# Hybrid trunk on one core: input quarters ahead of weight splits, and part of GpSimd's sine chain ahead of the first norm's factors

## The chip, the cores and the metric

The kernel runs on one core of a Trainium2 chip. The metric is the device time of one execution in microseconds; before the change it was 993.73 (median of three runs, 992.82 to 994.16). All times below are microseconds unless marked ns. TensorE is PE, VectorE is DVE, ScalarE is ACT, GpSimd is POOL, SyncE is SP, which issues most of the DMAs.

## The reference, cut to what matters

A decoder trunk of two layers over 256 tokens of width 1024, batch 1. Each layer is half a gated feed-forward block, a token mixer, and another half block:

```
for layer in range(2):
    h = h + 0.5 * swiglu(rms_norm(h, ffn_norm[layer, 0]), w_gate, w_up, w_down)
    h = h + mixer(rms_norm(h, mix_norm[layer]))        # layer 0: S5 state space, layer 1: block attention
    h = h + 0.5 * swiglu(rms_norm(h, ffn_norm[layer, 1]), w_gate, w_up, w_down)

rms_norm(x, g) = x * rsqrt(mean(x * x) + 1e-6) * g
swiglu(h)      = (silu(h @ w_gate) * (h @ w_up)) @ w_down          # inner width 2816
```

The S5 mixer needs tables that depend on its parameters alone. Two of their steps matter here:

```
dt  = exp(log_dt)
lam = exp(a_re * dt) * (cos(a_im * dt) + i * sin(a_im * dt))
```

and powers of lam after that.

## The kernel before

**Arithmetic.** All matrix products are float32 in three passes: a weight is split into a rounded part `whi` (ScalarE, line 84) and a rest `wlo` (VectorE, line 85), activations are split the same way into `xa` high and low halves, and TensorE adds high x high, low x high and high x low. Weights stream through three raw buffers of 1 MB (`Stream`, `RAW = 3`). A *unit* is 1 MB; it is split in two halves, numbered in order of use (split 0, 1, 2, ...). Only when both halves of a unit are split is its buffer free, and then SP issues the load of the unit three further on. `st.pump()` issues the next split if its data was asked for long enough ago.

**Order.** There is no scheduler: instructions go to each engine in the order in which the program text emits them, and each engine works through its queue in that order. Work for other engines is placed between the matmuls by lists of functions ("hooks") that run when the emission reaches a place.

**The front.** The first feed-forward half is `f00`. Its input x comes in four column *quarters* of 256. `quarter(q)` (line 1322) transposes a quarter on TensorE (line 1331, four transposes into PSUM tiles pA1 and pA3, one buffer each), scales and rounds it on ScalarE (line 1338, two instructions) and forms the rest on VectorE (line 1339, two instructions). The next quarter's transposes write the same two PSUM tiles, so they wait until VectorE has read the last ones. `gu0` (line 457) multiplies the quarters with the first gate and up weights: eight groups of six matmuls (line 471), for quarter q and token half t in the order (0,0), (0,1), (1,0), ..., (3,1). Ahead of each group it runs the hooks of `first` (line 1384), and then `fill(1.4)`, which moves a clock of slots and, from slot 9 on (that is from group (3,0)), advances the table generator `tab`.

**The norm.** The norm's factor is applied late. `square(t, n)` (line 1351) sums squares of half rows on ScalarE; after the fourth, `factors` (line 1355) makes the mean and x^-0.5 with one refinement step on GpSimd: seven instructions, lines 1356, 1357 and 304 to 308, result `rn`. In the product after gu0 (`gu(1, 0)`), `to_rows` (line 1361, ahead of its second group) transposes `rn` on TensorE, VectorE copies it, and `to_columns` (line 1368) transposes it back. Only then do `gated(0, 0)` and `gated(0, 1)` make the first activations (`sg` on ScalarE, line 478; `act` on VectorE, line 482), and `tr` transposes each (line 495) and splits it (`ah` line 497, `al` line 498).

**The tables.** `tables` (line 618) is a generator; each `next(tab)` emits its text to the next `yield`. Advance 1 is the exponent of dt on ScalarE (`dtb`, line 659). Advance 2 has three small transposes on TensorE (lines 662 to 664) and on VectorE the copy to `prm`, two reductions and `are` (lines 666 to 674). Advance 3 has `mag` and `rho` on ScalarE (lines 676, 677). Advance 4 has a transpose and copy for `dT` (lines 681, 682) and, on GpSimd through the helpers `pt` (line 685) and `pts` (lines 689, 691), the *sine chain*: fourteen instructions that reduce the angle and square it (lines 722 to 735: e0, e1, den, aim, q, y, y2), then the two polynomials `sc` (lines 736 to 743), then doublings (line 747) up to `s4`, `c4`. Later `e_init` (line 696) copies `c4` and `s4` on VectorE (lines 700, 701) into the power table `E`, and its steps (line 703, through line 626) follow, with splits between them. `pre` is eight loads of S5 parameters (`bn`, line 647), issued on SP at group (1,1).

Of the kernel before, what the change touches and what calls it, by code (L numbers as in the profile page):

```python
# [13 lines left out]
OP = mybir.AluOpType  # L14
# [11 lines left out]
TWO_PI = 2.0 * math.pi  # L26
MAGIC = 12582912.0
# [91 lines left out]
def trunk_kernel(ctx: ExitStack, tc, x, ffn_norm, ffn_w_gate, ffn_w_up, ffn_w_down, mix_norm,  # L119
# [3 lines left out]
    nc = tc.nc  # L123
# [13 lines left out]
    def psR():  # L137
        return pp.tile([128, 512], F32, name="pR", tag="R", bufs=2)

    def psA(i):  # L140
        return pp.tile([128, 512], F32, name=f"pA{i}", tag=f"A{i}", bufs=1)
# [93 lines left out]
    ident = cst[:, 0:128]  # L235
# [30 lines left out]
    if "s5" in phases:  # L266
# [5 lines left out]
        dnat = tabp.tile([8, 128], F32, name="dnat")  # L272
# [4 lines left out]
    st = Stream(nc, units, rp, hp)  # L277
# [37 lines left out]
    def home(pool, ph):  # L315

        xa = pool.tile([128, 4224], F32R, name="xa")
        v = xa[:, XO[ph]:XO[ph] + 4096].rearrange("p (i k c) -> p i k c", i=2, c=256)
        return v[:, 0], v[:, 1]
# [298 lines left out]
    def tables(tp):  # L618

        V, P = nc.vector, nc.gpsimd  # L620

        def T(name, *shape):
            return tp.tile([128] + list(shape), F32, name=name)
# [37 lines left out]
        ps = psR()  # L661
# [9 lines left out]
        dT = T("dT", 8)  # L671
        ar, ai, dt = prm[:, 0, :], prm[:, 1, :], prm[:, 2, :]
        are, aim, mag = T("are", 32), T("aim", 32), T("mag", 32)
# [1 line left out]
        yield  # L675
        nc.scalar.activation(mag, are, AF.Exp)
        nc.scalar.activation(rho, are, AF.Exp, scale=4.0)
        yield

        ps = psR()  # L680
        nc.tensor.transpose(ps[:, 0:8], dnat, ident[0:8, 0:8])
        V.tensor_copy(dT, ps[:, 0:8])

        def pt(o, a, b, op):
            P.tensor_tensor(o, a, b, op=op)  # L685

        def pts(o, a, s1, op0, s2=None, op1=None):
            if op1 is None:
                P.tensor_scalar(o, a, s1, None, op0=op0)
            else:  # L690
                P.tensor_scalar(o, a, s1, s2, op0=op0, op1=op1)

        z0, z1 = T("z0", 1024), T("z1", 1024)
        E = T("e", 2, 16, 65)
# [21 lines left out]
        def e_store(hf):  # L716
            nc.gpsimd.dma_start(dE[hf], E.rearrange("p i q c -> p (i q c)"))

        q, y, y2, e0, e1, den = (T(n, 32) for n in ("q", "y", "y2", "e0", "e1", "den"))
        sc = T("sc", 2, 32)  # L720
        sn, cs = sc[:, 0], sc[:, 1]
        pt(e0, ar, ar, OP.mult)
        pt(e1, ai, ai, OP.mult)
        pt(den, e0, e1, OP.add)
        pt(aim, ai, dt, OP.mult)
        pts(q, aim, 1.0 / TWO_PI, OP.mult, MAGIC, OP.add)
        pts(q, q, MAGIC, OP.subtract)
        c1 = 6.28125
        c2 = float(np.floor((TWO_PI - c1) * 2 ** 20) / 2 ** 20)
        c3 = TWO_PI - c1 - c2  # L730
        for k, c in enumerate((c1, c2, c3)):
            pts(e0, q, c, OP.mult)
            pt(y, y if k else aim, e0, OP.subtract)
        pts(y, y, 0.5, OP.mult)
        pt(y2, y, y, OP.mult)
        for k, n in enumerate(range(15, 1, -2)):
            if k:
                pt(sc, sc, cf7[:, k, :, None].to_broadcast([128, 2, 32]), OP.add)
# [562 lines left out]

    pre = []
    tab = tables(tabp) if "s5" in phases else iter(())
    next(tab, None)
    slot = [0]
# [16 lines left out]
    def quarter(q, mid=lambda: None):  # L1322

        if not X:
            X[phases[0], "x"] = True
            X["h"], X["l"] = home(XP[0], phases[0])
        pv = [psA(1 + 2 * k)[:, 0:256] for k in range(2)]
        for k in range(2):
            for t in range(2):
                c = (2 * q + k) * 128  # L1330
                nc.tensor.transpose(pv[k][:, t * 128:(t + 1) * 128].rearrange("p (s i) -> p i s", s=4),
                                    xn[t][:, c:c + 128], ident)
            if k == 0:
                mid()
        for k in range(2):
            g = gT[:, 2 * q + k:2 * q + k + 1]
            xh, xl = (X[p][:, 2 * q + k, :] for p in "hl")
            nc.scalar.activation(xh, pv[k], AF.Identity, scale=g)
            nc.vector.scalar_tensor_tensor(xl, pv[k], g, xh.bitcast(F32), op0=OP.mult, op1=OP.subtract)
# [11 lines left out]
    def square(t, n):  # L1351
        sq = sp.tile([128, 512], mybir.dt.bfloat16, name="sq", tag="sq", bufs=1)
        nc.scalar.activation(sq, xn[t][:, n * 512:(n + 1) * 512], AF.Square, accum_out=ss4[:, t, n:n + 1])
# [24 lines left out]
    ps = psR()  # L1378
    for a in ("h",) * 4 + ("l",) * 7:
# [1 line left out]
    st.pump()  # L1381
    next(tab, None)
    square(0, 0)
    first = {(0, 1): [st.pump, lambda: next(tab, None), lambda: quarter(1), lambda: square(1, 0)],
             (1, 0): [lambda: next(tab, None), lambda: quarter(2), st.pump, lambda: square(0, 1)],
             (1, 1): pre,
             (2, 0): [lambda: quarter(3), st.pump, lambda: square(1, 1), factors],
             (3, 0): [st.pump], (3, 1): [st.pump, lambda: warm(AF.Silu)]}
# [63 lines left out]
```

## Time and profile before

| | us |
|---|---|
| median of three runs | 993.73 (992.82 to 994.16) |
| the profiled execution | 993.93 |
| its span | 991.9 |
| TensorE busy | 973.8 (98%) |
| VectorE busy | 703.3 (71%) |
| ScalarE busy | 559.2 (56%) |
| GpSimd busy | 192.1 (19%) |

How to read the rows that follow. A timeline row has start, duration, engine, line of the kernel, operation, what it writes and reads, its shape and a count of merged instructions; in brackets stands the engine's idle time before it and what ended it. A waits row has the engine that waited and what for, then the sum, the number and the longest of these waits. A windows row has a stretch, its length, then busy time and instructions of PE, PE's weight loads, DVE, ACT and POOL, and then the granted TensorE clock, the share of the DMA engines and GB/s. The chain of work that ended last shows by which engines the span is bound:

```profile
PE 84%; DVE 7%; POOL 3%; issue 2%; ACT 2%; DMA 1%; SPq 0%; ACTq 0%; DVEq 0%; POOLq 0%
```

### The profile page before, as it was taken

The numbers are of one execution on the slowest core, as the hardware profiler recorded it, in microseconds if no ns is written. First come the engines' busy times: TensorE is split into PE (matmuls) and PEld (weight loads), VectorE is DVE, ScalarE is ACT, GpSimd is POOL, SyncE is SP. The second block draws the span as 40 slices with busy tenths as digits, with TensorE's granted clock in tenths as the row PEclk, the third lists the DMA queues.
The fourth block names the chain that finished last, engine by engine and source line by source line (L and its number), as shares of the span: only waits on it lengthen the run. The fifth ranks groups of instructions, "written<-read, shape, count | busy, mean of one in ns | idle before, by whom it ended". The sixth has DMA issues, their size and how long they took to land.

```text
span 991.9 us, 17175 instructions
## 1 busy us (share of the span) xinstructions
PE 973.8 (98%) x6695; PEld 866.0 (87%) x6695; DVE 703.3 (71%) x1148; ACT 559.2 (56%) x997; POOL 192.1 (19%) x361
## 2 busy tenths in 40 slices
PE   9999999999799999999999999999999999999998
PEld 7778888888687999999999999998888899999997
DVE  5799777768978776666667766665689667766662
ACT  6646666553255665555545555554898655655540
POOL 4882554414730100000010000000441010000000
PEclk9999999999999999999999999999999999999999
DMA  8978877886656565656536655554445446756531
GB/s 235 277 261 250 293 264 237 301 332 216 236 171 190 193 212 172 211 170 213 170 120 220 216 202 181 194 182 137 131 167 170 157 143 218 248 170 213 170 128 42
DMA packets 140000, 198.71 MB, mean 200 GB/s; under 512 B 18232, under 2 KB 111504, under 8 KB 139664
## 3 DMA queue, kind: packets, MB, share of 16 engines
q1 hardware_dynamic: 133808, 184.32, 56.2%
q0 software_dynamic: 5536, 12.71, 3.6%
q8 instruction: 52, 0.85, 0.4%
q10 hardware_dynamic: 576, 0.61, 0.3%
q14 instruction: 28, 0.23, 0.1%
HBM read 183.89 MB, written 13.66 MB: 199 GB/s over the span
## 4 chain that ended last, share of the span: by engine, by line
PE 84%; DVE 7%; POOL 3%; issue 2%; ACT 2%; DMA 1%; SPq 0%; ACTq 0%; DVEq 0%; POOLq 0%
PE pM L551 12%; PE pM L552 12%; PE pM L553 12%; PE pA L397 9%; PE pA L399 9%; PE pA L398 9%; PE pM L397 5%; PE pM L398 5%; PE pM L399 5%; DVE wlo L85 2%; DVE zo L1010 1%; POOL sc L685 1%; PE pR L331 1%; ACT whi L84 1%; PE pR L861 1%
## 5 line engine op out<-in xcount | busy, mean ns | idle before, releaser
L551 PE MATMUL pM<-xa,whi 128*128 128x256 f32 x1056 | 295.7, 280 | 0.0
L552 PE MATMUL pM<-xa,whi 128*128 128x256 f32 x1056 | 294.9, 279 | 0.0
L553 PE MATMUL pM<-xa,wlo 128*128 128x256 f32 x1056 | 294.7, 279 | 0.0
L91 DVE SCALAR_TENSOR_TENSOR wlo<-raw,gT,whi 128x512 fp32r<-128x512 f32 x328 | 228.2, 748 | 70.5 <-ACT whi L90 70.3
L85 DVE TENSOR_TENSOR wlo<-raw,whi 128x1024 fp32r<-128x1024 f32 (+1 forms) x157 | 191.4, 1234 | 55.6 <-ACT whi L84 54.7
L90 ACT ACTIVATE whi<-raw,gT 128x512 fp32r<-128x512 f32 x328 | 213.7, 711 | 19.6 <-PE pA L399 14.6
L552 PEld LDWEIGHTS pM<-xa,whi 128*128 128x128 f32 x1056 | 198.5, 188 | 2.6
L551 PEld LDWEIGHTS pM<-xa,whi 128*128 128x128 f32 x1056 | 198.5, 188 | 2.3
L553 PEld LDWEIGHTS pM<-xa,wlo 128*128 128x128 f32 x1056 | 198.5, 188 | 0.0
L84 ACT ACTIVATE whi<-raw 128x1024 fp32r<-128x1024 f32 (+1 forms) x157 | 161.1, 1049 | 29.1 <-PE pA L399 8.0
L397 PE MATMUL pA<-whi,ah 128*128 128x512 f32 x352 | 138.8, 394 | 0.0
L398 PE MATMUL pA<-wlo,ah 128*128 128x512 f32 x352 | 137.6, 391 | 0.0
L399 PE MATMUL pA<-whi,al 128*128 128x512 f32 x352 | 137.6, 391 | 0.0
L566 ACT ACTIVATE sg<-gr 128x256 f32<-128x256 f32 x66 | 27.6, 418 | 165.8 <-DVE gr L563 165.8
L397 PE MATMUL pM<-whi,xa 128*128 128x512 f32 x288 | 119.5, 415 | 0.0
L398 PE MATMUL pM<-wlo,xa 128*128 128x512 f32 x288 | 113.1, 393 | 0.1
L399 PE MATMUL pM<-whi,xa 128*128 128x512 f32 x288 | 112.7, 391 | 0.0
L346 POOL TENSOR_TENSOR ms<-ss 128x1 f32<-128x1 f32 x10 | 1.9, 193 | 472.1 <-ACT sq L343 472.1
L399 PEld LDWEIGHTS pA<-whi,al 128*128 128x128 f32 x352 | 66.1, 188 | 14.3
L397 PEld LDWEIGHTS pA<-whi,ah 128*128 128x128 f32 x352 | 66.1, 188 | 11.6
L398 PEld LDWEIGHTS pA<-wlo,ah 128*128 128x128 f32 x352 | 66.2, 188 | 11.3
L563 DVE TENSOR_TENSOR gr<-pM,rrow 128x512 f32<-128x512 f32 x66 | 45.5, 689 | 40.9 <-PE pM L553 40.8
(263 smaller groups left out, 1232.5 us busy)
## 6 DMA issues: line engine op xcount, KB each, us to landing
raw<-in_ffn_w_down_dram SPq DMA_DIRECT2D x44, 1024.0 KB, 5.2
raw<-in_ffn_w_gate_dram SPq DMA_DIRECT2D x80, 512.0 KB, 3.8
raw<-in_ffn_w_up_dram SPq DMA_DIRECT2D x80, 512.0 KB, 4.9
raw<-in_moba_w_qkv_dram SPq DMA_DIRECT2D x12, 1024.0 KB, 5.1
TB<-dB SPq DMA_DIRECT2D x8, 768.0 KB, 6.0
raw<-in_ffn_w_gate_dram SPq DMA_DIRECT2D x16, 256.0 KB, 4.2
raw<-in_ffn_w_up_dram SPq DMA_DIRECT2D x16, 256.0 KB, 4.7
dB<-tt POOLq DMA_DIRECT2D x16, 256.0 KB, 6.0
```

What stands on the lines that cost most here:

```text
L84: nc.scalar.activation(hi[:, c], r[:, c], AF.Copy)
L85: nc.vector.tensor_tensor(lo[:, c], r[:, c], hi[:, c].bitcast(F32), op=OP.subtract)
L90: nc.scalar.activation(hi[:, c], r[:, c], AF.Identity, scale=g)
L91: nc.vector.scalar_tensor_tensor(lo[:, c], r[:, c], g, hi[:, c].bitcast(F32), op0=OP.mult, op1=OP.subtract)
L397: mm(o, xh, wh, start=start, stop=False)
L398: mm(o, xh, wl, start=False, stop=False)
L399: mm(o, xl, wh, start=False, stop=stop)
L551: mm(o, a, xh, start=k == 0 and i == 0, stop=False, skip_group_check=True)
L552: mm(o, a, xl, start=False, stop=False, skip_group_check=True)
L553: mm(o, b, xh, start=False, stop=k == 7, skip_group_check=True)
L563: V.tensor_tensor(gr, ps.rearrange("p (i c) -> p i c", i=2), Rr["row"][:, None, :].to_broadcast([128, 2, 256]), op=OP.mult)
L566: nc.scalar.activation(sg, gr[:, 0, :], AF.Silu)
```

## The change

It moves emission, nothing else. The first fourteen instructions of the sine chain, with the tiles that they need, move from advance 4 to the end of advance 3 of the table generator. In `first`, quarter 1 goes from the third to the first place ahead of group (0,1), so ahead of a split and of table advance 2; and ahead of group (1,0) table advance 3 goes from the first place to the last, behind quarter 2, a split and a square. Since advance 3 is emitted ahead of group (1,0) and `factors` ahead of group (2,0), the fourteen instructions now stand ahead of the seven of the factors in GpSimd's queue; before they stood behind them.

```diff
         nc.scalar.activation(mag, are, AF.Exp)
         nc.scalar.activation(rho, are, AF.Exp, scale=4.0)
-        yield
-
-        ps = psR()
-        nc.tensor.transpose(ps[:, 0:8], dnat, ident[0:8, 0:8])
-        V.tensor_copy(dT, ps[:, 0:8])
 
         def pt(o, a, b, op):
...
-        z0, z1 = T("z0", 1024), T("z1", 1024)
-        E = T("e", 2, 16, 65)
...
         q, y, y2, e0, e1, den = (T(n, 32) for n in ("q", "y", "y2", "e0", "e1", "den"))
         sc = T("sc", 2, 32)
...
             pt(y, y if k else aim, e0, OP.subtract)
         pts(y, y, 0.5, OP.mult)
         pt(y2, y, y, OP.mult)
+        yield
+
+        ps = psR()
+        nc.tensor.transpose(ps[:, 0:8], dnat, ident[0:8, 0:8])
+        V.tensor_copy(dT, ps[:, 0:8])
+
+        z0, z1 = T("z0", 1024), T("z1", 1024)
+        E = T("e", 2, 16, 65)
...
         for k, n in enumerate(range(15, 1, -2)):
             if k:
                 pt(sc, sc, cf7[:, k, :, None].to_broadcast([128, 2, 32]), OP.add)
...
-    first = {(0, 1): [st.pump, lambda: next(tab, None), lambda: quarter(1), lambda: square(1, 0)],
-             (1, 0): [lambda: next(tab, None), lambda: quarter(2), st.pump, lambda: square(0, 1)],
+    first = {(0, 1): [lambda: quarter(1), st.pump, lambda: next(tab, None), lambda: square(1, 0)],
+             (1, 0): [lambda: quarter(2), st.pump, lambda: square(0, 1), lambda: next(tab, None)],
              (1, 1): pre,
              (2, 0): [lambda: quarter(3), st.pump, lambda: square(1, 1), factors],
```

More of the change, by code (lines that the diff above doesn't have):

```diff
@@ L691, in pts @@
                 P.tensor_scalar(o, a, s1, s2, op0=op0, op1=op1)
+        q, y, y2, e0, e1, den = (T(n, 32) for n in ("q", "y", "y2", "e0", "e1", "den"))
+        sc = T("sc", 2, 32)
+        sn, cs = sc[:, 0], sc[:, 1]
+        pt(e0, ar, ar, OP.mult)
+        pt(e1, ai, ai, OP.mult)
+        pt(den, e0, e1, OP.add)
+        pt(aim, ai, dt, OP.mult)
+        pts(q, aim, 1.0 / TWO_PI, OP.mult, MAGIC, OP.add)
+        pts(q, q, MAGIC, OP.subtract)
+        c1 = 6.28125
+        c2 = float(np.floor((TWO_PI - c1) * 2 ** 20) / 2 ** 20)
+        c3 = TWO_PI - c1 - c2
+        for k, c in enumerate((c1, c2, c3)):
+            pts(e0, q, c, OP.mult)
+            pt(y, y if k else aim, e0, OP.subtract)
+        pts(y, y, 0.5, OP.mult)
+        pt(y2, y, y, OP.mult)
+        yield
+        ps = psR()
+        nc.tensor.transpose(ps[:, 0:8], dnat, ident[0:8, 0:8])
+        V.tensor_copy(dT, ps[:, 0:8])
         z0, z1 = T("z0", 1024), T("z1", 1024)
@@ L717, in e_store @@
             nc.gpsimd.dma_start(dE[hf], E.rearrange("p i q c -> p (i q c)"))
[L719 to L735, printed above, removed]
         for k, n in enumerate(range(15, 1, -2)):
```

## The prediction

> **What bounds the kernel now.** I read the page first, then TensorE's waits, then its timeline, and then the engines that it waits for.
>
> ```profile
> PE 973.8 (98%) x6695; PEld 866.0 (87%) x6695; DVE 703.3 (71%) x1148; ACT 559.2 (56%) x997; POOL 192.1 (19%) x361
> ...
> PE pR L495 <- DVE act L482: 1.7, 2, 1.4
> PE pA L1331 <- DVE xa L1339: 1.2, 1, 1.2
> ...
> PE pR L293 <- DVE al L498: 0.5, 1, 0.5
> ```
>
> TensorE (PE) is busy for 98% of the span, and only three kinds of wait in the first half layer are counted here (beside the first of all, for the ones tile). So in the front the change can win or lose only what PE stands still. Its timeline shows where:
>
> ```profile
> 13.22 0.83 PE L1331 MATMUL pA<-cst,xn 128*128 128x128 f32 x4 [1.16 <-DVE xa L1339]
> 13.81 1.18 PE L471 MATMUL pA<-whi,xa 128*128 128x512 f32 x4
> ...
> 23.18 0.39 PE L398 MATMUL pM<-wlo,xa 128*128 128x512 f32 x1
> 23.41 0.39 PE L399 MATMUL pM<-whi,xa 128*128 128x512 f32 x1
> 23.81 0.27 PE L1364 MATMUL pR<-cst,rn 128*2 128x128 f32 x1
> ...
> 34.10 0.44 PE L495 MATMUL pR<-cst,act 128*128 128x128 f32 x2 [0.29 <-DVE act L482]
> ...
> 52.60 0.44 PE L495 MATMUL pR<-cst,act 128*128 128x128 f32 x2 [1.39 <-DVE act L482]
> ...
> 59.96 0.39 PE L399 MATMUL pM<-whi,xa 128*128 128x512 f32 x1
> 60.42 0.63 PE L821 MATMUL pR<-cst,cn 128*64 128x128 f32 x4
> ...
> 68.10 0.23 PE L293 MATMUL pR<-cst,gm 16*128 16x16 f32 x1 [0.47 <-DVE al L498]
> ```
>
> A 128x512 matmul is drawn 0.39 us long, but the next one follows it by 0.23 (23.18, 23.41). So a standstill is the idle time in brackets plus 0.16, or start less (last start + 0.23). Six of them: **A** 11.90 to 13.22, 1.32 us (third input quarter); **B** 23.64 to 23.81, 0.17 (to_rows waits for the norm factors rn); **C** 33.65 to 34.10, 0.45; **D** 51.05 to 52.60, 1.55; **E** 60.19 to 60.42, 0.23; **F** 67.47 to 68.10, 0.63. The other waits of the list are in the S5 stage and after, so a shift of PE at 68.10 is a shift of the end.
>
> Where D, E and F come from, VectorE (DVE) and GpSimd (POOL) show:
>
> ```profile
> 45.56 0.23 DVE L700 COPY e<-c 128x16 f32<-128x16 f32 x1 [3.85 <-POOL c L691]
> ...
> 23.70 0.43 POOL L685 TENSOR_TENSOR e<-prm 128x32 f32<-128x32 f32 x2
> 24.22 1.42 POOL L685 TENSOR_TENSOR den<-e,e 128x32 f32<-128x32 f32 x1
> ...
> 30.53 0.29 POOL L685 TENSOR_TENSOR sc<-y,cf 128x64 f32<-128x64 f32 x1
> ...
> 42.38 0.25 POOL L685 TENSOR_TENSOR sc<-sc,y 128x32 f32<-128x32 f32 x1
> ...
> 45.31 0.22 POOL L691 TENSOR_SCALAR c<-e 128x32 f32<-128x32 f32 x1
> ```
>
> The sine chain starts behind the factors at 23.70 and gives c at 45.53. DVE stands 3.85 us at L700, from 41.7; splits, act and al are queued behind it, and
>
> ```profile
> 51.00:69.00 18.00, 16.07 (x79) 12.63 (x79) 17.97 (x29) 9.59 (x17) 17.61 (x33) 1.00 0.70 235
> ```
>
> shows DVE (third figure) without a gap for 18 us: it pays the 3.85 us back slowly, and PE waits for act (D) and for PSUM banks that al has to free (E, F).
>
> **The change, part by part.** No instruction is added or removed. That z0, z1 and E lie 1 KB further on in the table pool (seven small tiles are now allocated ahead of them) I cost at nothing; no row tells of it.
>
> *Quarters ahead of splits and table steps.* Quarter 1 (4 transposes, 2 ScalarE, 2 DVE instructions) goes ahead of split 1 on ScalarE and DVE, and ahead of the three table transposes on PE and the prm/gm/are steps on DVE.
>
> ```profile
> 9.69 1.06 ACT L84 ACTIVATE whi<-raw 128x1024 fp32r<-128x1024 f32 x1 [0.58 <-DMA raw<-in_ffn_w_up_dram]
> ...
> 9.73 0.25 PE L662 MATMUL pR<-cst,scn 32*128 32x32 f32 x1
> ...
> 10.78 1.23 DVE L85 TENSOR_TENSOR wlo<-raw,whi 128x1024 fp32r<-128x1024 f32 x1 [1.68 <-ACT whi L84]
> 11.92 0.25 DVE L666 COPY prm<-pR 128x96 f32<-128x96 f32 x1
> ...
> 12.69 0.87 DVE L1339 SCALAR_TENSOR_TENSOR xa<-pA,gT,xa 128x256 fp32r<-128x256 f32 x2
> ...
> 12.03 0.37 SPq L173 DMA_DIRECT2D raw<-in_ffn_w_gate_dram  x1
> ```
>
> DVE's quarter work ran from 12.69 to 13.56 because 1.23 (split) and 0.77 (11.92 to 12.69, table) stood ahead. Without them ScalarE can start the quarter at about 10.2, half a microsecond behind its transposes, which take the slot of the table's transposes at 9.73; DVE starts at 10.7 and is done at 11.6, before PE asks at 11.90. A goes: the matmuls of 13.81 start at 12.2 or 12.3, 1.5 to 1.6 us earlier. The price: split 1 starts at about 10.9 instead of 9.69, its DVE half ends at 13.2 instead of 12.01, just when PE needs it (12.3 + 4 x 0.23 = 13.2; at most 0.1 lost). Behind that DVE half waits SP's next raw load, 12.03 becomes 13.2, with the bn loads and the first down block behind it on the queue. I cost that at nothing: the DMA engines' share is 0.98 between 8 and 23 us (row below), so a transfer has work queued in front of it. Without this cover, 1.2 us. prm moves from 11.92 to 13.15.
>
> *Table step behind split and square.* mag and rho (two ScalarE instructions) go behind a split; their reader on POOL comes after c, so they cost nothing. PE then keeps its lead of about 1.6 us to the end of its front stage, with quarters 2 and 3 ready in time. In the order of the new queues, with 1.06 for a split on ScalarE, 1.23 on DVE, 0.87 for a quarter on either: ScalarE has square, quarter 2 (12.6), split 2 (13.4), square, mag and rho, quarter 3 (15.5), split 3 (16.2), the last square (17.2 to 18.0), splits 4 and 5; DVE has prm to are (13.15 to 13.9), quarter 2 (to 14.8), splits 2 (14.7 to 15.9), 3 (17.3 to 18.6), 4 and 5 (18.9 to 21.3). PE's eight groups of six matmuls (6 x 0.23 = 1.38 each) then end at 21.2 and the first group of the next product at 21.9: that is when PE reaches to_rows, instead of at 23.64.
>
> *Fourteen POOL instructions ahead of the factors.* This decides.
>
> ```profile
> 19.54 0.61 POOL L1356 TENSOR_TENSOR ms<-ss 128x2 f32<-128x2 f32 x1 [12.29 <-ACT sq L1353]
> ...
> 24.32 1.20 DVE L85 TENSOR_TENSOR wlo<-raw,whi 128x1024 fp32r<-128x1024 f32 x1
> ...
> 25.60 0.25 POOL L685 TENSOR_TENSOR aim<-prm 128x32 f32<-128x32 f32 x1
> ...
> L304 POOL TENSOR_TENSOR rr<-ms,nhalf x10: 548/554/877, 216.4 to 806.8; 128x1 f32<-128x1 f32 x10
> ```
>
> The factors start when the last square is done (19.54) and take some 4.2 us, to the first chain row at 23.70. With PE's lead that square would be done at about 18.0. But now the fourteen instructions stand ahead; they start behind prm, at 13.45, and took 30.53 - 23.70 = 6.83 us, so they end at 20.28, and the factors with their old 4.2 at 24.5. That is the first estimate of rn. The second goes instruction by instruction: free, one takes about 0.36 us with its gap; one that meets a DVE split lasts till the split's end (den 1.42 beside the split at 24.32, aim free 0.25). The four splits just listed let the fourteen through by about 21.8; then DVE itself waits for rn, and the factors run free: six at 0.28 and the pow at an estimated 0.7 for two columns (0.55 for one, last row), 2.4 us, so rn at 24.2. Bounds from rows: fourteen free instructions (5.0) let the factors start at 18.5 and end at 20.9; fourteen at the rate of the sc rows (30.53 to 42.38, fourteen in 11.85 us, seven splits) end at 25.3, and rn at 29.5. I take 24.2 to 24.5, since four splits, not seven, fall in the window. So PE's lead of 1.6 us is lost again at to_rows, and it leaves there 0.4 to 0.7 us later than 23.81.
>
> What that delay costs is read from C. The next stop on PE is act at 34.10, and that is set by another chain:
>
> ```profile
> 24.22 0.54 SPq L179 DMA_DIRECT2D raw<-in_ffn_w_down_dram  x1
> ...
> 29.70 1.06 ACT L84 ACTIVATE whi<-raw 128x1024 fp32r<-128x1024 f32 x1 [3.02 <-DMA raw<-in_ffn_w_down_dram]
> ...
> 8.00:23.00 15.00, 13.84 (x68) 10.47 (x67) 10.48 (x18) 12.18 (x26) 3.12 (x4) 1.00 0.98 272
> ```
>
> ScalarE waits 3.02 us for the first down block, issued at 24.22 and landed at 29.7; activations and splits are queued behind it, and through them the act that releases 34.10. The transfers before it are bound by the DMA engines, so this does not move. C covers 0.45 of PE's delay of 0.4 to 0.7: net 0 to 0.28 at 34.10. The same chain would swallow an earlier rn too.
>
> *The rest of the chain.* Part two starts at about 24.3 instead of 30.53, 6.2 us sooner, and c comes at 38 to 39.5 against the 41.7 at which DVE asks. The 3.85 us go, and the act that releases 52.60 comes some 3.5 us sooner, before 51.05: D goes (1.55). PE is then 1.78 earlier at F, DVE over 3: E and F go too (0.23 + 0.63). What is late next are PE's own releases of split buffers, which move with it.
>
> Sum: 1.55 + 0.23 + 0.63 = 2.41, less 0 to 0.28 at C: 2.1 to 2.4. The profiled execution took 993.93 us (span 991.9), so it would take 991.5 to 991.8. The median of the runs, 993.73, is 0.2 lower; I put **991.5**, own range 991.1 to 992.0.
>
> **The clock.** PE will stand about 2.3 us at to_rows (21.9 to 24.2). What a standstill does, the S5 stage shows:
>
> ```profile
> 246.07 0.40 PE L1043 MATMUL pR<-hr,TB 128*64 128x64 f32 x8
> 252.64 0.69 PE L1059 MATMUL pR<-cst,gs 128*128 128x128 f32 x2 [3.97 <-DVE gs L1050]
> 253.60 0.64 PE L1043 MATMUL pR<-hr,TB 128*64 128x64 f32 x8
> 256.09 0.44 PE L1059 MATMUL pR<-cst,gs 128*128 128x128 f32 x2
> ...
> 271.39 0.44 PE L1059 MATMUL pR<-cst,gs 128*128 128x128 f32 x2 [2.28 <-ACT gf L1063]
> 271.92 0.40 PE L1043 MATMUL pR<-hr,TB 128*64 128x64 f32 x8
> ```
>
> After 3.97 us of waiting, eight matmuls take 0.64 instead of 0.40 up to 256.09, about half speed for 3.45 us, a loss of 1.7; after 2.28 us nothing is lost. The border lies between, and 2.3 is at its lower end. [...]
>
> **The rivals.**
> 1. *The standstill trips the clock.* For it: 2.3 to 2.6 us of standing are above the 2.28 seen as harmless. Against: far nearer to it than to 3.97. PE loses 1.7 more than C covers: 993.2 to 993.5. [...]
> 2. *Only D goes.* DVE still has its splits to do and is behind PE at F: gain 1.55 less 0 to 0.28, 992.4 to 992.7. Against: 3.85 us less queued work.
> [...]
> 4. *Slower: factors starved.* Place: L308's rn, behind fourteen instructions that DVE's splits hold up. At the sc rows' rate rn comes at 29.5: 5.2 beyond C's cover, 1.7 for the clock, and part two starts only 1.0 earlier, so most of the 2.41 is missing: 998.4 to 1000.8. It decides from rn = 25.9 (idle 3.97): 1.6 + 1.7 against 2.41, 994.8.
> 5. *The quarters do nothing at the end and nothing else does either* (c still late, for instance because blocked instructions multiply): 993.9, as before.
>
> **How the numbers follow.** Forecast 0.55, rival 1 0.11, rival 2 0.14, rival 3 0.08, rival 4 0.07, rival 5 0.05. The range 989.6 to 993.6 takes in rivals 1, 2 and 3 and leaves out 4 and 5, together 0.12. A measurement of this kernel tells about 0.2% (2.0 us, 991.7) from no change. The forecast's range lies mostly below that: with rival 3, faster 0.54; same 0.39 from the rest of the forecast and rivals 1, 2, 5; slower 0.07.
>
> **What would show it.** Right: no wait of pA transposes for xa near 12 us; a new wait of PE at the rn transpose of 2 to 2.6 us, ended by POOL near 24.2 to 24.5; first act stop still near 34.1 behind the down block's landing near 29.7; c before 40; DVE without the 3.85 us; no stop at 51, and the gm transpose about 2.3 us earlier. Wrong: rn after 25.9, half-speed matmuls behind it, a down block that lands later than 29.7 (then C grows by as much), or act still late near 51.

## The result, and the profile after

| | before | after |
|---|---|---|
| median (lowest to highest) | 993.63 (992.82 to 994.41), 16 runs | 991.66 (991.20 to 992.18), 16 runs |
| ratio, 95% interval | | 0.998, 0.9972 to 0.9988 |
| span of the profiled execution | 991.9 | 990.0 |

The changed kernel is 1.97 faster, which is the 0.2% that the measurement can just tell; the highest run of after lies below the lowest of before. In the changed program most lines have one more than before (L1331 is L1332, L1059 is L1060), and the chain's helpers stand elsewhere (L685 is L680, L689 is L684, L691 is L686, L700 is L718).

The waits of TensorE in the changed kernel, all that its list has (sum, number, longest):

```profile
PE pR L1060 <- DVE gs L1051: 4.0, 1, 4.0
PE pR L1060 <- ACT gf L1064: 3.4, 2, 1.9
PE pR L1365 <- POOL rn L308: 1.6, 1, 1.6
PE pR L1346 <- POOL ones L227: 1.0, 1, 1.0
PE pR L495 <- DVE act L482: 0.7, 1, 0.7
PE pA L397 <- DVE xa L1092: 0.2, 1, 0.2
```

Against the list of before, the wait for xa (1.2) and that for al (0.5) are gone, act has one wait of 0.7 instead of two with 1.7, and a new one is there: 1.6 for rn. TensorE's timeline shows where, at the places of A, the reach of to_rows, B, C and F:

```profile
11.79 0.60 PE L1332 MATMUL pA<-cst,xn 128*128 128x128 f32 x4
12.15 1.18 PE L471 MATMUL pA<-whi,xa 128*128 128x512 f32 x4
...
21.77 0.39 PE L399 MATMUL pM<-whi,xa 128*128 128x512 f32 x1
23.75 0.27 PE L1365 MATMUL pR<-cst,rn 128*2 128x128 f32 x1 [1.59 <-POOL rn L308]
...
34.39 0.44 PE L495 MATMUL pR<-cst,act 128*128 128x128 f32 x2 [0.66 <-DVE act L482]
...
66.00 0.23 PE L293 MATMUL pR<-cst,gm 16*128 16x16 f32 x1
```

TensorE is at the third quarter 1.4 earlier, reaches to_rows at 22.0 (21.77 + 0.23), stands there until 23.75 and so has nothing left of its lead. The gm transpose of 68.10 comes at 66.00 and waits for nothing. Start times matched one to one between the two traces give the shift along the way:

| place | before | after | shift |
|---|---|---|---|
| third quarter's transposes (A) | 13.22 | 11.79 | -1.43 |
| rn transpose (B) | 23.81 | 23.75 | -0.06 |
| first act (C) | 34.10 | 34.39 | +0.29 |
| second act (D) | 52.60 | 51.34 | -1.26 |
| cn transposes (E) | 60.42 | 58.86 | -1.56 |
| gm transpose (F) | 68.10 | 66.00 | -2.11 |
| S5, second wait | 271.39 | 269.25 | -2.14 |
| S5, end of the next stretch | 280.48 | 279.82 | -0.66 |
| behind the S5 stage | 298.30 | 296.52 | -1.78 |

GpSimd's timeline, with the first of the fourteen instructions and the last, the four that a split held up, the factors and c:

```profile
13.21 0.45 POOL L680 TENSOR_TENSOR e<-prm 128x32 f32<-128x32 f32 x2 [5.96 <-DVE prm L666]
...
14.59 1.24 POOL L684 TENSOR_SCALAR q<-q 128x32 f32<-128x32 f32 x1
15.91 0.30 POOL L684 TENSOR_SCALAR e<-q 128x32 f32<-128x32 f32 x1
...
17.35 1.26 POOL L684 TENSOR_SCALAR e<-q 128x32 f32<-128x32 f32 x1
...
19.04 1.14 POOL L684 TENSOR_SCALAR y<-y 128x32 f32<-128x32 f32 x1
20.26 1.07 POOL L680 TENSOR_TENSOR y<-y 128x32 f32<-128x32 f32 x1
21.30 0.19 POOL L1357 TENSOR_TENSOR ms<-ss 128x2 f32<-128x2 f32 x1
...
23.49 0.20 POOL L308 TENSOR_TENSOR rn<-rn,rs_e 128x2 f32<-128x2 f32 x1
...
37.49 0.21 POOL L686 TENSOR_SCALAR c<-e 128x32 f32<-128x32 f32 x1
```

The factors rn are there at 23.69, the tile `c` at 37.70. The timelines of SP (issue of the first down block), ScalarE and VectorE:

```profile
24.46 0.53 SPq L179 DMA_DIRECT2D raw<-in_ffn_w_down_dram  x1
...
30.04 1.06 ACT L84 ACTIVATE whi<-raw 128x1024 fp32r<-128x1024 f32 x1 [3.41 <-DMA raw<-in_ffn_w_down_dram]
...
41.69 0.19 DVE L718 COPY e<-c 128x16 f32<-128x16 f32 x1
...
48.30 0.47 DVE L482 SCALAR_TENSOR_TENSOR act<-pM,rr,sg 128x256 f32<-128x256 f32 x1
```

VectorE copies c at 41.69 without the 3.85 of idle time, four microseconds after c was ready, and the act that held up 52.60 is done at 48.8. The windows row of the stretch in which VectorE had no gap before now has PE without one (18.00 of 18.00, first figure):

```profile
51.00:69.00 18.00, 18.00 (x90) 14.58 (x89) 17.33 (x28) 10.73 (x18) 15.10 (x27) 1.00 0.79 271
```

### The profile page after: what moved, and what is told of

Its sections match the earlier page's. It is cut to its first block, busy times and chain, and to the rows that moved or that the text cites. A ratio compares the mean times of both kernels' runs of the same rounds, so it can differ in the third digit from the quotient of the medians.

```text
span 990.0 us, 17176 instructions
## 1 busy us (share of the span) xinstructions
PE 974.4 (98%) x6695; PEld 868.0 (88%) x6695; DVE 702.8 (71%) x1148; ACT 559.7 (57%) x997; POOL 192.4 (19%) x361
## 4 chain that ended last, share of the span: by engine, by line
PE 89%; DVE 5%; issue 2%; POOL 1%; DMA 1%; ACT 1%; DVEq 0%; ACTq 0%; POOLq 0%; SPq 0%
PE pM L552 12%; PE pM L551 12%; PE pM L553 12%; PE pA L397 10%; PE pA L399 10%; PE pA L398 9%; PE pM L397 6%; PE pM L398 6%; PE pM L399 6%; DVE zo L1011 1%; PE pR L331 1%; DMA raw<-in_ffn_w_up_dram 1%; DVE wlo L85 1%; PE pR L862 1%; DVE zi L1008 1%
```

## The experiments

Each was timed beside the kernel before, on the same chip. The question behind the first two was which part of the change brings the gain, behind the next ones what bounds it: the down block (C), the length of the part that stands ahead of the factors, and TensorE's clock in S5.

### e1_quarters_only

The kernel before, with the new lists of `first` alone.

```diff
-    first = {(0, 1): [st.pump, lambda: next(tab, None), lambda: quarter(1), lambda: square(1, 0)],
-             (1, 0): [lambda: next(tab, None), lambda: quarter(2), st.pump, lambda: square(0, 1)],
+    first = {(0, 1): [lambda: quarter(1), st.pump, lambda: next(tab, None), lambda: square(1, 0)],
+             (1, 0): [lambda: quarter(2), st.pump, lambda: square(0, 1), lambda: next(tab, None)],
```

> Only the new order of the hooks (quarters ahead of splits and table steps); the fourteen chain instructions stay behind the factors. Theory (the gain comes from when GpSimd delivers c, the lead of the quarters itself is swallowed by the stop at act, which the first down block sets): TensorE's wait for xa near 12 us goes, rn comes near 22.1 and TensorE leaves to_rows 1.6 us earlier, but its stop at act still ends at 34.1 to 34.4 and is about 2.2 us long; the chain starts 1.6 us earlier, VectorE's wait for c is about 2.2 instead of 3.85 us, and the gain is what VectorE wins there, 1.6 us: 992.0 (to 992.4). Rival (the quarters carry their lead to the end): the stop at act moves to 32.6 and the gain is 1.5 us before anything of the chain, 991.0 or less.

Measured: 992.33 (991.84 to 993.44, 11 runs) against 993.57, ratio 0.9984 (0.9976 to 0.9993). Its timelines of ScalarE, TensorE and VectorE have

```profile
29.42 1.06 ACT L84 ACTIVATE whi<-raw 128x1024 fp32r<-128x1024 f32 x1 [4.29 <-DMA raw<-in_ffn_w_down_dram]
...
33.97 0.44 PE L495 MATMUL pR<-cst,act 128*128 128x128 f32 x2 [1.72 <-DVE act L482]
...
44.08 0.22 DVE L700 COPY e<-c 128x16 f32<-128x16 f32 x1 [2.65 <-POOL c L691]
```

Here rn comes early (the transpose of 23.81 stands at 22.26), and C swallows the whole lead: TensorE waits 1.72 for act and starts only 0.13 earlier. At 52.60 it is nevertheless 1.46 earlier. The earlier factors let the chain start earlier, so VectorE gets c at 44.08 instead of 45.56, 1.48 sooner, and stands 2.65 instead of 3.85. The quarters alone gain through c, not through their own lead.

### e2_chain_only

The changed kernel's tables, with the old lists of `first`.

```diff
-    first = {(0, 1): [lambda: quarter(1), st.pump, lambda: next(tab, None), lambda: square(1, 0)],
-             (1, 0): [lambda: quarter(2), st.pump, lambda: square(0, 1), lambda: next(tab, None)],
+    first = {(0, 1): [st.pump, lambda: next(tab, None), lambda: quarter(1), lambda: square(1, 0)],
+             (1, 0): [lambda: next(tab, None), lambda: quarter(2), st.pump, lambda: square(0, 1)],
```

> Only the chain's fourteen instructions ahead of the factors; the hooks in the order of before. Theory (the chain is the whole gain): TensorE still waits 1.2 us for xa at 13.2 and rn comes at 23.7 to 24.0 as before; VectorE's wait for c is gone, the stops at 52, 60 and 68 us too; 991.2 (to 991.7), as fast as the changed kernel or a little faster. Rival (both parts share the gain): 992.5 or more.

Measured: 991.60 (990.85 to 991.64, 7 runs), ratio 0.9972 (0.9961 to 0.9982). A row of its list of waits, then its timelines of GpSimd and VectorE:

```profile
PE pA L1332 <- DVE xa L1340: 0.8, 1, 0.8
```

```profile
18.96 0.63 POOL L1357 TENSOR_TENSOR ms<-ss 128x2 f32<-128x2 f32 x1 [1.93 <-ACT sq L1354]
...
41.06 0.20 DVE L718 COPY e<-c 128x16 f32<-128x16 f32 x1
```

The wait for the third quarter stays (0.8), and the result is that of the whole change: TensorE is 2.68 earlier at 68.10, and 2.24 behind S5. With the old lists prm is early enough for the fourteen instructions to end before the last square: the factors even wait 1.93 for it. So the part on the chain is sufficient for the gain, and the quarters add nothing to it that the runs can tell. The two gains do not add up: from the act of 34.10 to 68.10, the stretch with D, E and F, the quarters alone gain 1.3, the chain alone 2.3 and both together 2.4. Both go through c, and once c is there before VectorE asks, sooner is worth nothing. That e2's profile is 0.57 further ahead at 68.10 than the changed kernel's (2.68 against 2.11) comes from the act, where e2 is 0.34 earlier than the kernel before and the changed kernel 0.29 later; how far such a difference can be trusted is said below, under C.

### e3_bn_late

C is set by the first down block, which SP issues behind the eight loads of `bn`. This kernel issues those loads later, behind the second down block.

```diff
+    extra[:0] = [(18.0 + 0.6 * i, lambda i=i: pre[i]()) for i in range(8)]
...
-             (1, 1): pre,
```

> The changed kernel with the eight small bn loads issued behind the first two down blocks instead of at group (1,1). Theory (the stop at act is set by the landing of the first down block, which stands behind the bn loads on SyncE's queue): that block is issued near 18.5 and lands near 24 to 25, ScalarE doesn't wait for it, the stop at 34.4 (0.83 us) goes: 990.8. Rival (the stop is made by the queues of ScalarE and VectorE themselves): it stays, 991.7.

Measured: 994.98 (993.16 to 996.84, 12 runs), ratio 1.0011 (1.0002 to 1.002): not faster, but, just clear of the noise, slower. The rows are of its profiled execution, which took 993.16, the lowest of the twelve; first the timelines of SP and ScalarE, then the windows:

```profile
18.03 0.37 SPq L179 DMA_DIRECT2D raw<-in_ffn_w_down_dram  x1
...
51.39 2.01 ACT L84 ACTIVATE whi<-raw 128x1024 fp32r<-128x1024 f32 x2 [5.58 <-DMA raw<-in_ffn_w_up_dram]
```

```profile
51.00:69.00 18.00, 16.09 (x78) 12.37 (x77) 16.32 (x26) 11.48 (x20) 9.61 (x24) 1.00 0.93 313
```

The guess about C is right: with the down block issued at 18.03 instead of 24.46 the act of 34.10 comes at 33.12, and at 52.60 TensorE is 2.62 ahead of the kernel before. But the moved loads now meet the weight stream later: the DMA engines' share from 51 to 69 rises to 0.93 (0.79 in the changed kernel), ScalarE waits 5.58 for a weight block, TensorE waits 1.0 for al, and at 68.10 only 0.93 is left. Why the median run took 1.8 more than this one, no profile shows.

### e4_bn_late_cut8

The same, and in addition only eight of the fourteen instructions ahead of the factors.

```diff
             pt(y, y if k else aim, e0, OP.subtract)
+            if k == 0:
+                yield
         pts(y, y, 0.5, OP.mult)
         pt(y2, y, y, OP.mult)
-        yield
```

> As e3_bn_late, and only eight of the fourteen chain instructions ahead of the factors. Theory (the lead of the quarters is lost at to_rows because the factors stand behind fourteen instructions, and then at act because of the down block): rn comes near 22.1, TensorE leaves to_rows 1.5 us earlier than in the changed kernel and nothing holds it at act: 0.8 + 1.5 less than 991.7, 989.4. Rival (another wait takes their place before 50 us, a raw block or VectorE): 990.3 to 990.8.

Measured: 993.48 (992.01 to 994.57, 11 runs), ratio 0.9993 (0.9985 to 1.0002). The act of 34.10 comes at 31.90, 2.20 earlier, and 52.60 is 3.81 earlier; by 68.10 the late loads have taken that down to 2.03, with a wait of 1.1 for `cb` (made from the late loads) on TensorE. The shorter part ahead of the factors pays, the late loads do not.

### e5_more_ahead

The other way: seven more instructions of the chain ahead of the factors, the first polynomial steps.

```diff
+        for k in range(4):
+            sc_step(k)
         yield
...
-        for k, n in enumerate(range(15, 1, -2)):
...
+        for k in range(4, 7):
+            sc_step(k)
```

> The changed kernel with seven more chain instructions (the first four steps of the polynomials) ahead of the factors, so twenty-one in all. Theory (a late rn costs TensorE one for one beyond the 0.8 us of cover at act, and the chain's end stays early enough): rn comes 2.6 us later, near 26.3, TensorE stands about 4.3 us at to_rows, 1.8 us come through and the clock falls to half for some 3.4 us, 1.7 more: 993.5 without the clock, 995.2 with it. Rival (the cover at act takes all of it): 991.7.

Measured: 996.01 (994.36 to 996.25, 9 runs) against 993.67, ratio 1.0021 (1.0012 to 1.0031). TensorE's timeline behind to_rows:

```profile
26.90 0.27 PE L1371 MATMUL pR<-cst,rn 128*2 128x128 f32 x1 [4.28 <-POOL rn L308]
...
27.70 0.39 PE L397 MATMUL pM<-whi,xa 128*128 128x512 f32 x1
...
29.66 0.63 PE L398 MATMUL pM<-wlo,xa 128*128 128x512 f32 x1
...
31.61 0.39 PE L397 MATMUL pM<-whi,xa 128*128 128x512 f32 x1
```

This is rival 4 with rival 1 behind it; the time is 0.8 above the 995.2 expected. The factors come 3.1 later than before, and 0.8 after TensorE went on the matmuls are still drawn at 0.39, then at 0.63 until past 30.5, and at 0.39 again by 31.61: the shift grows from 3.1 to 4.6 over the slow stretch, which at 3.4 (27.92 to 31.36) is as long as the one of 3.45 that the S5 rows of before show. C has long been passed: the act of 34.10 stands at 38.24, 4.14 later. The freed c gives the usual gain back, but at 68.10 the kernel is still 1.68 behind. In the changed kernel, with 1.59 of waiting at the same place, no matmul behind it is drawn longer, and the granted clock is 1.00 from 23.75 to 30.00.

### e6_keep_clock and e9_one_fill

These ask what TensorE's clock in the S5 stage is worth. Both add matmuls on the ones tile into an unused part of a PSUM tile, ahead of transposes which wait there: extra work, its result unread. The first puts 12, 5 and 6 of them ahead of three waits, the second 12 ahead of the first wait alone.

```diff
+            for _ in range({0: 12, 3: 5, 4: 6}.get(b, 0)):
+                mm(ps[:, 256:384], ones, ones, start=True, stop=True)
```

> The changed kernel with 12, 5 and 6 matmuls without use in front of three waits of the S5 stage (g_tr 0, 3 and 4), so that TensorE stands less. Theory (0.3 us of the gain were lost because TensorE ran at half clock behind its third wait of the S5 stage): granted clock 1.00 in the whole stage, the shift at the end of the stage is as large as at its beginning, 991.3. Rival (VectorE's chain sets the stage, the clock costs nothing): 991.7.

```diff
             if b == 0:
                 GT["h"], GT["l"] = home(xp, "g")
+                for _ in range(12):
+                    mm(ps[:, 256:384], ones, ones, start=True, stop=True)
```

> The changed kernel with 12 matmuls without use ahead of the first long wait of the S5 stage alone (g_tr 0); in e6_keep_clock those ahead of g_tr 3 and 4 waited for a PSUM bank themselves and made TensorE late. Theory (the half clock behind the 4 us wait costs the stage some 0.9 us, which carried to 268 us in e6_keep_clock): 990.8. Rival (the stage's later waits are set by VectorE and ScalarE and take it up): 991.7.

Measured: e6 992.28 against 993.67 (11 runs, seven from 991.28 to 992.55 and four from 993.26 to 994.28), ratio 0.999 (0.9981 to 0.9999); e9 991.53 (991.02 to 993.20, 11 runs) against 993.88, ratio 0.9979 (0.997 to 0.9988), no better than the change itself with its 0.998. The windows of the same stretch, first the changed kernel, then e9:

```profile
245.00:258.00 13.00, 9.02 (x181) 7.91 (x177) 12.38 (x29) 3.24 (x10) 9.94 (x10) 0.74 0.88 328
```

```profile
245.00:258.00 13.00, 11.62 (x208) 10.71 (x209) 12.37 (x27) 3.63 (x10) 9.95 (x10) 1.00 0.85 317
```

And from e9's timeline of TensorE:

```profile
268.86 0.44 PE L1062 MATMUL pR<-cst,gs 128*128 128x128 f32 x2 [3.14 <-ACT gf L1066]
```

The granted clock goes from 0.74 to 1.00, and at the matmuls that the kernel before starts at 256.46 TensorE is 3.72 ahead of it, where the changed kernel is 1.89 ahead. Then it waits 3.14 at 268.86 where the changed kernel waits 1.46, and the lead is back at 2.52, about what this profile had at 68.10 already (2.49). VectorE works 12.4 of these 13 us in both, and the wait at 268.86 ends with ScalarE's tile `gf`: the stage goes by their work, and a faster TensorE only waits longer. In e6 the extra matmuls of a later wait were themselves held (3.1, until `gf`), so it does not show more.

### e7_down_first and e8_down_first_cut8

What e3 and e4 taught, put together: the `bn` loads stay in the front, but directly behind the first down block, not in front of it; e8 also has the cut of e4.

```diff
-             (1, 1): pre,
-             (2, 0): [lambda: quarter(3), st.pump, lambda: square(1, 1), factors],
+             (2, 0): [lambda: quarter(3), st.pump, lambda: square(1, 1), factors] + pre,
```

> The changed kernel with the bn loads issued directly behind the first down block (at group (2,0)) instead of ahead of it (at (1,1)); the moved loads of e3_bn_late collided with later blocks, these don't. Theory (the stop at act is set by the down block behind the bn loads): the block is issued near 18.5 and lands near 24, the stop at 34.4 (0.83 us) goes, nothing later gets worse: 990.8. Rival (any place for the bn loads costs a raw block as much somewhere else before 70 us): 991.7 or more.

> As e7_down_first, and only eight of the fourteen chain instructions ahead of the factors. Theory (with both the late factors and the late down block gone the quarters' lead comes through): TensorE leaves to_rows near 22.2 and has no stop at act, 1.5 us better than e7_down_first, 989.3. Rival (VectorE or a raw block stops TensorE before 70 us instead): 990.3 to 991.

Measured against 993.88 (993.20 to 994.85, 16 runs): e7 991.07 (990.69 to 991.61, 7 runs), ratio 0.9973 (0.9961 to 0.9984); e8 **989.80** (989.54 to 990.12, 5 runs), ratio 0.996 (0.9947 to 0.9973). In e7 ScalarE splits the down block at 26.50 without a wait for it, and TensorE's act row is

```profile
33.55 0.38 PE L495 MATMUL pR<-cst,act 128*128 128x128 f32 x2
```

without idle time: C is gone. The `bn` loads do no harm here: the DMA engines' share from 51 to 69 is 0.81 in e8, where e3 had 0.93, and up to 55 ScalarE in e7 waits 2.6 at most for a weight block. What is left is the late rn. E8's timelines of GpSimd and TensorE:

```profile
17.78 0.63 POOL L1358 TENSOR_TENSOR ms<-ss 128x2 f32<-128x2 f32 x1 [1.32 <-ACT sq L1355]
...
21.81 0.20 POOL L308 TENSOR_TENSOR rn<-rn,rs_e 128x2 f32<-128x2 f32 x1
22.06 0.27 PE L1366 MATMUL pR<-cst,rn 128*2 128x128 f32 x1
...
31.89 0.38 PE L495 MATMUL pR<-cst,act 128*128 128x128 f32 x2
...
39.13 1.29 POOL L686 TENSOR_SCALAR c<-e 128x32 f32<-128x32 f32 x1
```

Eight instructions end before the last square, so the factors wait for the square alone. They are there at 22.01, when TensorE comes, and the lead of the quarters reaches the act (31.89, 2.21 earlier than before; 2.20 in e4), and this time TensorE has not lost it again by 68.10. The tile `c` now comes at 40.4 instead of 37.7, which costs nothing, since VectorE copies it at 41.46. At 68.10 TensorE is 4.13 ahead, and the span is 4.1 shorter (987.8): 2.2 are there at the act (the lead of 1.7 and the 0.45 of C), the other 1.9 come at D, E and F. This version beats both kernels: its slowest run lies below the fastest of the changed one (990.12, 991.20).

## Why the prediction was right, and where it was not

**Quarters.** A went, as worked out: matmuls at 12.15 (12.2 to 12.3), to_rows reached at 22.0 (21.9). Split 1's delay and with it SP's raw load, 12.98 instead of 12.03 (13.2 predicted), were costed at nothing. The down block was issued 0.24 later (24.46), and e1, e6 and e9, whose raw loads were about as late (13.08, 13.29, 12.91), issued it at 23.92, 23.40 and 24.05, before the 24.22 of the kernel before: the date of the raw load does not set it one for one, which agrees with the cover by queued transfers (the DMA engines' share from 8 to 23 is 0.97 in the changed kernel and 1.00 in e1).

**Fourteen instructions ahead of the factors.** The walk instruction by instruction was the right estimate, the sum of old durations less so. Four splits did fall in the window, four instructions were held (1.24, 1.26, 1.14 and 1.07), and the fourteen took 8.1 (13.21 to 21.33; 13.45 to 21.8 predicted). The factors then ran free in 2.4 (21.30 to 23.69), as worked out. So rn was 0.5 to 0.8 earlier than the 24.2 to 24.5 forecast, half a microsecond of it in the fourteen, whose start alone was 0.24 early. So TensorE left to_rows 0.06 earlier than before, not 0.4 to 0.7 later.

**C.** The net of +0.29 at 34.10 is the upper end of the 0 to 0.28 forecast, but not for its reason, so that the agreement here is luck. The factors were not late. The down block's first split started at 30.04 instead of 29.70, 0.34 later, where the prediction says "this does not move", and TensorE's standstill before the act grew from 0.45 to 0.66 + 0.16 = 0.82. The prediction had named this (C then grows by as much). That the down block sets C is shown by e7, where issuing it first removes the stop. But the 0.34 need not be the work of the change. E6 and e9 differ from the changed kernel only from the S5 stage on, and in their profiles the same split starts earlier. The timeline of ScalarE, first e6, then e9:

```profile
29.00 1.06 ACT L84 ACTIVATE whi<-raw 128x1024 fp32r<-128x1024 f32 x1 [2.05 <-DMA raw<-in_ffn_w_down_dram]
```

```profile
29.64 1.06 ACT L84 ACTIVATE whi<-raw 128x1024 fp32r<-128x1024 f32 x1 [3.08 <-DMA raw<-in_ffn_w_down_dram]
```

There the act of 34.10 comes at 33.91, without a wait, and at 34.00. So one and the same front differs by 1.0 at this split and by 0.5 at the act from execution to execution, and a single pair of profiles does not tell whether the change moves the block at all.

**The rest of the chain.** The tile `c` at 37.70 was a little sooner than the 38 to 39.5 forecast, and VectorE asked at 41.69 as before. D, E and F went, exactly: +0.29 - 2.41 = -2.12, and the trace has -2.11 at 68.10. E6 and e9, with the same front, gain 2.5 and 2.4 between the act and 68.10, so this part of the sum does not hang on the one profile. Rival 2 (only D goes) and rival 5 fell with that; e2 shows that this part is enough for the whole gain.

**The clock.** Rival 1 did not come: 1.59 in brackets at to_rows, and a granted clock of 1.00 behind it (23.75 to 30.00). TensorE stood there 1.75, not the 2.3 of the forecast; that 2.3 would be harmless was an estimate from the 2.28 in S5, and it was not tested. Rival 4 did not come, and e5 shows that its mechanism is there, one step of size away. Rival 3, with 0.08 among the chances, stands for S5 without its clock drop. No run shows how near its 3.97 of waiting is to a wait without a drop; behind 3.98 the drop came again. In the profiled execution the opposite of the rival happened: the first drop lasted longer, and a second came. In the first the granted clock is 0.51 in the kernel before (252.6 to 256.1) and 0.50 in the changed one (250.7 to 254.5). Behind it a row of 32 matmuls runs at 1.00 in the kernel before (256.1 to 258.0), but still partly at half speed in the changed one (0.65 from 254.5 to 256.5), which starts it 1.89 earlier. TensorE's timeline, first of the kernel before, then of the changed one:

```profile
256.46 1.15 PE L985 MATMUL pM<-U,TA 128*64 128x64 f32 x32
```

```profile
254.57 1.74 PE L986 MATMUL pM<-U,TA 128*64 128x64 f32 x32
```

This takes the lead from 2.14 to 1.31, and the next wait, 1.46 instead of 2.28, gives it back. Behind the second drop (granted clock 0.57 from 276 to 280) the lead fell from 2.14 to 0.66, of which 1.1 came back by 296.5, so 0.36 of it was lost for good. Over the 16 runs the price is small: those with a granted clock of 0.998 (four) took 991.21 to 991.80, median 991.47, those with 0.995 (ten) 991.20 to 992.00, median 991.71.

**The number.** 991.5 was forecast, 991.66 measured. The terms D, E and F and their places were right. At C two errors (rn 0.5 to 0.8 sooner, down block 0.34 later) cancelled, by luck. The prediction took a shift at 68.10 for a shift of the end; the 0.36 lost in S5 is missing there, and explains why the profile's gain is 1.9 and not 2.1. The gain of the medians, 1.97, lies a little under the 2.1 to 2.4 of the sum as well.

The prediction did not ask what the quarters are worth beside the chain. The runs answer: in this change nothing that they can tell (e2 without them 0.9972, the change 0.998, intervals that overlap), since rn, behind fourteen instructions, takes their lead away again; in e8, with eight, the lead of 1.7 is kept. No run tried e8 without them.

## What to carry to other kernels

Two reorderings that gain by way of the same late result don't add up: find the date at which the result is asked for, and move only as much work ahead of others as meets it (here eight instructions rather than fourteen, with c at 40.4 against 41.46). When several small loads stand in front of a large one on an issuing queue, look at what waits for the large one first; here moving it ahead was free (e7, 991.07) where moving the small ones far back was not (e3, 994.98). In e9 a standstill filled on an engine that is not the stage's bound came back as a longer wait later in the stage: 3.14 instead of 1.46, some 16 us on.

## What the runs showed of the hardware

**The same wait, another clock.** In the S5 stage both kernels run the same matmuls up to a wait of almost the same length, 6.95 us after the wait before it. First the kernel before, then the changed one, from TensorE's timeline; then the windows of the one and of the other:

```profile
278.34 0.44 PE L1059 MATMUL pR<-cst,gs 128*128 128x128 f32 x2 [1.95 <-ACT gf L1063]
...
278.87 0.40 PE L1043 MATMUL pR<-hr,TB 128*64 128x64 f32 x8
```

```profile
276.20 0.56 PE L1060 MATMUL pR<-cst,gs 128*128 128x128 f32 x2 [1.94 <-ACT gf L1064]
...
276.96 0.64 PE L1044 MATMUL pR<-hr,TB 128*64 128x64 f32 x8
```

```profile
274.00:284.00 10.00, 8.05 (x115) 7.45 (x114) 7.63 (x17) 4.21 (x8) 6.47 (x6) 1.00 0.33 107
```

```profile
272.00:282.00 10.00, 8.06 (x90) 7.45 (x89) 7.63 (x17) 4.36 (x8) 6.30 (x6) 0.83 0.33 107
```

After 1.95 the eight matmuls take 0.40, after 1.94 they take 0.64, with a granted clock of 0.83 over the ten microseconds. So in these two profiles the length of the last wait doesn't decide, nor do the last two together (the wait before was 2.28 in the kernel that kept its clock and 1.46 in the one that lost it), and the prediction's border, between 2.28 and 3.97, isn't one. In e5 the matmuls slowed down only 1 us or so after work went on at 26.90, behind 4.28 of waiting: they are drawn 0.39 up to 27.70 and 0.63 from 28.31. Runs of one kernel differ as well: the 16 runs of the changed one have granted clocks of 0.995 to 0.998. What decides, no trace here shows.

**GpSimd beside a split.** In the changed kernel the four of the fourteen instructions that start beside a VectorE split last until 0.09 to 0.16 behind the split's end, where the others take 0.22 to 0.30: `q` took 1.24 from 14.59, beside this split of VectorE's timeline, which ends at 15.67:

```profile
14.45 1.22 DVE L85 TENSOR_TENSOR wlo<-raw,whi 128x1024 fp32r<-128x1024 f32 x1
```

Beside the quarters' VectorE instructions from 15.93, which read one input from PSUM, nothing is held (0.30 from 15.91). Why the two differ, the trace does not show; what a split cost these four is its remaining time. The power instruction of the factors took 1.72 from 20.53 in the kernel before, beside splits at 20.44 and 21.66 of 1.22 each, and 0.74 from 21.85 in the changed kernel, where VectorE stands idle from 21.24.
